# Alternating large and small expert pairs, with a rearranged beginning and end of a mixture-of-experts stage

## The chip, the core and the metric

One core of a Trainium2 chip runs the whole program in one launch. The metric is the device time of one execution in microseconds (us). The engines named below are TensorE (PE in the profile, its weight loads PEld), VectorE (DVE), ScalarE (ACT), GpSimd (POOL) and SyncE (SP), whose queue issues most transfers. SBUF holds tiles of 128 partitions; matmuls write to the eight banks of PSUM.

## What is computed

A model of several layers works on 256 tokens of width 1024, in float32. The change concerns its last stage alone, a mixture of 32 experts with the final norm, cut here to what matters:

```python
logits = hf @ router_w + router_b
top_logit, top_idx = lax.top_k(logits, 4)
gates = softmax(top_logit)                      # 4 experts for each of 256 tokens
gu = x_rows @ w_gu[e] + b_gu[e]                 # 1024 -> 2048
gate, up = min(gu[..., :1024], 7), clip(gu[..., 1024:], -7, 7)
y = ((up + 1) * gate * sigmoid(1.702 * gate)) @ w_down[e] + b_down[e]
x = x + g2 * segment_sum(y * row_gate, row_tok)
out = rms_norm(x) * final_g
```

Every expert's weights are read once: 8.4 MB of w_gu and 4.2 MB of w_down, 402.7 MB for 32 experts.

## The kernel before, in words

`run` (at the end of the file) computes the layers one after another; `moe` (L2077) is the last. All its weights are loaded by SP's queue with `wload` (L146 to L156) into one ring of 16 buffers of about 1 MB (`big`), in the order of the program: eight tiles of w_gu and four of w_down for an expert, 24 tiles for a pair. A buffer is loaded again when the matmuls that read it are done.

The experts are ranked by how many tokens chose them (`moe_route`, L2364), and each rank has a fixed number of rows: experts 0 and 1 come first with 64 rows each, then ranks 2 to 8 with 96, ranks 9 to 16 with 64, ranks 17 to 31 with 32. `pairs` (L2086) puts two ranks together that share one set of up to 128 rows: pair 0 is experts 0 and 1, whose weights are loaded before the ranks are known (`first`, L2089); pairs 1 to 7 are 96 + 32 rows (called large below), pairs 8 to 15 are 64 + 32 (small). They run in this order. An expert's number is read from the tile `orders` into a register of SP (`moe_expert`, L2322), for the address of its weights.

For a pair, `pair` (L2236) makes a matrix that picks the pair's tokens, `gather` (L2197) multiplies it with the normalized tokens, held as a high and a low part (`xn`, made at L2268 to L2271 through a raw copy `xnraw` in the tile `moey`), and ScalarE and VectorE in turn scale the result into `xg`. `up` (L2129) adds the bias with matmuls of a selecting matrix `sel` (L2139 to L2145), which needs the ranks, and then multiplies by w_gu (L2154, recorded as L2126); L2161 to L2165 compute the activation, `down` (L2178) transposes it and multiplies by w_down (also L2126), and L2195 multiplies by the gate vector `moegate`, which `gate_bc` spreads over the partitions (L2110). `put` (L167 to L176) scales the rows by the token's weight and splits them into two parts, `scatter` (L2112) adds them to the residual `X` with matmuls (L2119) and additions (L2121). It runs one pair late. A rank with more tokens than rows is handled by `moe_beyond` (L2324): a branch on all engines over a long body, which reads a flag from `orders` (L2327) and in the measured run is not taken (L2328). In the body stand weight loads into the same ring, matmuls, activations and additions to `X`. After it the final norm: squares (L400), logarithm and exponential (L110, L111) with their activation table preloaded (L2310, recorded as L101), product (L2315) and the write of the output (L2316).

What the order of the instructions is: the tile framework schedules them per engine by what it takes to be ready first, so an instruction without operands can float up; `keep_in_program_order` holds one behind the instruction of its engine traced just before it in the same block. Waits between engines are put in by the framework, by tile. Four PSUM banks rotate under the name `mm`, four under `tp`, in the order in which the program takes them.

Of the kernel before, what the change touches and what calls it, by code (L numbers as in the profile page):

```python
# [50 lines left out]
class Kern:  # L51
# [2025 lines left out]
    def moe(self):  # L2077
# [7 lines left out]

        pairs = [((0, 64), (1, 64))] + [((1 + b, 96 if b < 8 else 64), (32 - b, 32)) for b in range(1, 16)]  # L2086
        rows = dict(chain.from_iterable(pairs))
        most = lambda r: 256 if r < 2 else min(256, 1024 // (r - 1))
        first = [gu_of(0), dn_of(0), gu_of(1)]  # L2089
        with self.pool("moe", 1) as P, self.pool("moew", 1) as W:  # L2090
# [18 lines left out]
            bgu = [P.tile([128, 512], F32, name=f"bgu{i}") for i in "hl"]  # L2109
            gate = self.gate_bc(P, 2, 5, 0, "moegate", tc.keep_in_program_order)  # L2110

            def scatter(gt, ys):  # L2112

                for t in range(2):
                    for h in range(2):
                        hs = slice(h * 512, h * 512 + 512)
                        p = self.ps("tp")
                        for i, v in enumerate(ys):
                            nc.tensor.matmul(p, gt[:, t * 128:(t + 1) * 128], v[:, hs], start=(i == 0), stop=(i == len(ys) - 1))  # L2119
                        x = self.X(2 + t)[:, hs]  # L2120
                        nc.vector.tensor_add(x, x, p)  # L2121
                        yield
# [5 lines left out]

            def up(gu, r, xs):  # L2129


                ps = []
                for x in xs:
                    n = x.shape[2]
                    w = 8 * n
                    pair = [self.ps("mm"), self.ps("mm")]
                    ps.append(pair)
                    sel = W.tile([128, 2, 160], F32, name="moesel", bufs=2)[:, :, :takes[n].shape[2]]
                    nc.gpsimd.tensor_scalar(sel.bitcast(FR), takes[n], own[:, r:r + 1], None, op0=OP.mult)  # L2139
                    for q, p in enumerate(pair):  # L2140
                        for j in range(64 // n):
                            m0 = 0 if n == 64 else 32 - 32 * j
                            for i in range(2):
                                nc.tensor.matmul(p[:, :w], sel[:, q, m0:m0 + 128].bitcast(FR),  # L2144
                                                 bgu[i][:, j * w:(j + 1) * w].bitcast(FR), start=(i == j == 0), stop=False)  # L2145
                step = 8 // len(xs) // 2 if len(xs) > 1 else 8
                for k0 in range(0, 8, step):
                    for x, pair in zip(xs, ps):
                        n = x.shape[2]
                        w, mm = tile_mm(n)  # L2150
                        for k in range(k0, k0 + step):
                            for p, c0 in zip(pair, (0, D)):
                                for c in range(128 // n):
                                    mm(p, c, x[:, k, :], gu(k)[:, c0 + c * w:c0 + (c + 1) * w], False, k == 7)  # L2154
                us = []
# [41 lines left out]
            def gather(x, oh, n):  # L2197

                per = 4 if n > 64 else 8
                for k0 in range(0, 8, per):  # L2200
                    p = self.ps("tp")
                    pv = p[:, :per * n].rearrange("p (k s) -> p k s", k=per)
                    for kk in range(per):
                        ks = slice((k0 + kk) * 128, (k0 + kk + 1) * 128)
                        for i, v in enumerate(xn):
                            for t in range(2):
# [29 lines left out]
            def pair(b):  # L2236
# [5 lines left out]
                for r, n in pairs[b]:  # L2242
                    nc.vector.tensor_tensor(oh[:, :, r0:r0 + n].bitcast(FR), bc(io[:, None, 0:n], [128, 2, n]),
                                            bc(ps_[:, :, r:r + 1], [128, 2, n]), op=OP.is_equal)
                    r0 += n
                xg = W.tile([128, 8, 128], F32, name="xg", bufs=2)[:, :, :m]
                gather(xg, oh, m)
# [16 lines left out]
            with self.pool("moer", 1) as T:  # L2264
# [3 lines left out]
                for t in range(2):  # L2268
                    xr = W.tile([128, D], F32, name="xnraw", tag="moey")
                    nc.scalar.activation(xr, self.X(2 + t), AF.Copy, scale=self.rx[:, t:t + 1])  # L2270
                    self.split(xr, xn[0][:, t, :], xn[1][:, t, :])  # L2271
                route = self.moe_route(T, W, io, pos0, R0, pos, R, G, Ge, own, takes, orders, rows)
# [3 lines left out]
                next(route)  # L2276
                self.split(braw, *bgu)
                gt, tg = next(cur)
            back = iter(())
            for b in range(16):  # L2280
                if b == 1:
                    self.moe_bias(W, Ge, gate)
                y, yh, yl = (W.tile([128, D], F32, name=f"moey{i}")[:sum(n for _, n in pairs[b])] for i in ("", "h", "l"))
                row = 0
                for i, (r, n) in enumerate(pairs[b]):
# [3 lines left out]
                    row += n  # L2289
                    us = up(gu, r, [xg[:, :, q] for q in rs])  # L2290

# [6 lines left out]
                    down(dn, us, [y[q] for q in rs])  # L2298
                self.put((yh, yl), y, tg[:, 1:2])
                back = scatter(gt.bitcast(FR), [yh.bitcast(FR), yl.bitcast(FR)])  # L2300
# [3 lines left out]
            fg = W.tile([128, D], F32, name="fing", tag="moey")  # L2304
            nc.sync.dma_start(fg, bass.AP(tensor=a["final_g_2"].tensor, offset=a["final_g_2"].offset, ap=[[0, 128], [1, D]]))
            for _ in back:
                pass
            self.moe_beyond(rows, most, orders, gu_of, dn_of, overflow)

            self.ln_exp()  # L2310
            with self.pool("moef", 1) as F:
                xs = [self.X(2), self.X(3)]
                r = self.row_rms(F, xs)
                for t in range(2):
                    nc.vector.scalar_tensor_tensor(xs[t], xs[t], r[:, t:t + 1], fg, op0=OP.mult, op1=OP.mult)  # L2315
                    nc.sync.dma_start(a["out"][t * 128:(t + 1) * 128], xs[t])  # L2316

# [237 lines left out]
```

## Time and profile before

| | us |
|---|---|
| median of 3 runs (lowest, highest) | 3098.86 (3097.3, 3103.04) |
| profiled execution, its own time | 3102.66 |
| its span, first to last instruction | 3100.9 |
| TensorE busy | 2765.1 (89%), mean granted clock 0.916 |
| VectorE busy | 1490.4 (48%) |
| ScalarE busy | 882.5 (28%) |
| GpSimd busy | 517.4 (17%) |
| transfers | 650.74 MB, mean 210 GB/s |

Times count from the start of the span. A busy TensorE is not TensorE at its peak: its matmuls overlap, and their ends are modelled. The granted clock is a share of 2.4 GHz, averaged over a stretch; single instructions run at 1.2 or 2.4 GHz. The DMA share is the mean over 16 engines and goes a little over 1 where packets overlap. A wait is put down to what released it last. A line can be a helper's.

### The profile page before, as it was taken

The numbers are of one execution on the slowest core, as the hardware profiler recorded it, in microseconds if no ns is written. First come the engines' busy times: TensorE is split into PE (matmuls) and PEld (weight loads), VectorE is DVE, ScalarE is ACT, GpSimd is POOL, SyncE is SP. The second block draws the span as 40 slices with busy tenths as digits, with TensorE's granted clock in tenths as the row PEclk, the third lists the DMA queues.
The fourth block names the chain that finished last, engine by engine and source line by source line (L and its number), as shares of the span: only waits on it lengthen the run. The fifth ranks groups of instructions, "written<-read, shape, count | busy, mean of one in ns | idle before, by whom it ended". The sixth has DMA issues, their size and how long they took to land. (4 is left out here: it accounts for less than half of the span.)

```text
span 3100.9 us, 47594 instructions
## 1 busy us (share of the span) xinstructions
PE 2765.1 (89%) x19070; PEld 1795.3 (58%) x19070; DVE 1490.4 (48%) x3210; ACT 882.5 (28%) x1827; POOL 517.4 (17%) x774
## 2 busy tenths in 40 slices
PE   7998989999979788987899988989999999998775
PEld 4873468888847555654798966763444433443332
DVE  4426465555567655764655878651222222222121
ACT  4223334223235343433454634530100000000001
POOL 0002310111100543543100322111100000000000
PEclk9998999999988897887899998989999999879887
DMA  6226741233221233432456323369999999999997
GB/s 227 96 92 211 273 144 55 95 95 95 86 86 42 75 108 98 108 95 81 144 190 204 118 62 113 125 248 360 381 411 382 373 377 372 416 417 416 416 417 290
DMA packets 254007, 650.74 MB, mean 210 GB/s; under 512 B 68816, under 2 KB 129616, under 8 KB 215376
## 3 DMA queue, kind: packets, MB, share of 16 engines
q1 hardware_dynamic: 239552, 632.96, 55.4%
q10 hardware_dynamic: 12432, 10.45, 1.1%
q0 software_dynamic: 1792, 4.20, 0.5%
q8 instruction: 152, 2.49, 0.3%
q14 instruction: 79, 0.65, 0.1%
HBM read 639.16 MB, written 8.39 MB: 209 GB/s over the span
## 5 line engine op out<-in xcount | busy, mean ns | idle before, releaser
L2126 PE MATMUL mm<-w,xg 128*32 128x256 f32 (+1 forms) x3904 | 434.2, 457 | 38.3 <-DMA w<-in_moe_w_gu_dram 38.3
L164 DVE TENSOR_TENSOR lo<-w,hi 128x512 fp32r<-128x512 f32 (+1 forms) x330 | 295.1, 927 | 107.7 <-ACT hi L163 93.4
L2126 PEld LDWEIGHTS mm<-w,xg 128*32 128x32 f32 (+1 forms) x3904 | 155.7, 120 | 306.0 <-issue 190.2
L163 ACT ACTIVATE hi<-w 128x512 fp32r<-128x512 f32 (+1 forms) x356 | 256.3, 770 | 236.5 <-PE tp L250 101.2
L2126 PE MATMUL mm<-w,moeaT 128*32 128x256 f32 (+1 forms) x1952 | 258.7, 500 | 8.7 <-DVE moeaT L95 3.8
L2162 ACT ACTIVATE moes<-moeg 128x256 f32<-128x256 f32 (+1 forms) x39 | 19.9, 510 | 653.6 <-DVE moeg L2161 653.6
L2161 DVE TENSOR_SCALAR moeg<-mm 128x256 f32<-128x256 f32 (+1 forms) x39 | 21.1, 541 | 349.7 <-PE mm L2126 349.3
L250 PE MATMUL mm<-mlo,hi 128*128 128x512 f32 (+1 forms) x512 | 173.4, 339 | 0.7 <-DVE mlo L173 0.7
L249 PE MATMUL mm<-mhi,hi 128*128 128x512 f32 (+1 forms) x512 | 173.1, 340 | 0.0
L251 PE MATMUL mm<-mhi,lo 128*128 128x512 f32 (+1 forms) x512 | 172.2, 337 | 0.0
L2126 PEld LDWEIGHTS mm<-w,moeaT 128*32 128x32 f32 (+1 forms) x1952 | 79.8, 128 | 140.8 <-issue 108.8
L251 PE MATMUL tp<-hi,aTl 128*128 128x512 f32 x384 | 151.7, 395 | 0.0
L250 PE MATMUL tp<-lo,aTh 128*128 128x512 f32 x384 | 151.3, 394 | 0.0
L249 PE MATMUL tp<-hi,aTh 128*128 128x512 f32 x384 | 151.1, 393 | 0.0
L2164 POOL TENSOR_TENSOR moeg<-moeg,moes 128x256 f32<-128x256 f32 (+1 forms) x39 | 37.4, 959 | 580.6 <-ACT moes L2162 566.0
L2195 DVE TENSOR_TENSOR moey<-mm,moegate 32x256 f32<-32x256 f32 (+1 forms) x122 | 60.5, 496 | 138.8 <-PE mm L2126 127.3
L164 POOL TENSOR_TENSOR lo<-w,hi 128x512 fp32r<-128x512 f32 (+1 forms) x26 | 51.8, 1994 | 348.0 <-ACT hi L163 293.9
L250 PEld LDWEIGHTS mm<-mlo,hi 128*128 128x128 f32 x512 | 96.4, 188 | 12.8 <-DVE mlo L173 1.1
L249 PEld LDWEIGHTS mm<-mhi,hi 128*128 128x128 f32 x512 | 96.0, 188 | 12.3 <-issue 0.5
L251 PEld LDWEIGHTS mm<-mhi,lo 128*128 128x128 f32 x512 | 96.3, 188 | 11.4
L2139 POOL TENSOR_SCALAR moesel<-moetk,moeown 128x320 fp32r<-128x320 f32 (+1 forms) x39 | 40.8, 1046 | 317.3 <-PE mm L2144 278.0
L249 PE MATMUL cv<-hT2h,hi 128*128 128x256 f32 x288 | 84.3, 293 | 8.8 <-DVE cvy L1754 8.8
(866 smaller groups left out, 5897.8 us busy)
## 6 DMA issues: line engine op xcount, KB each, us to landing
w<-in_moe_w_gu_dram SPq DMA_DIRECT2D x256, 1024.0 KB, 15.0
w<-in_moe_w_down_dram SPq DMA_DIRECT2D x128, 1024.0 KB, 16.6
w<-in_mlp_w_dram SPq DMA_DIRECT2D x64, 1024.0 KB, 5.4
w<-in_ada_w_dram SPq DMA_DIRECT2D x48, 1024.0 KB, 5.0
w<-in_w_in_dram SPq DMA_DIRECT2D x26, 1024.0 KB, 5.2
adaw<-in_ada_w_dram SPq DMA_DIRECT2D x48, 512.0 KB, 4.1
w<-in_ab_w_in_dram SPq DMA_DIRECT2D x14, 1024.0 KB, 5.1
w<-in_rw_w_rkv_dram SPq DMA_DIRECT2D x8, 1024.0 KB, 5.1
```

Source lines behind the costliest of these rows:

```text
L163: nc.scalar.activation(h, raw, AF.Copy)
L164: (eng or nc.vector).tensor_sub(l, raw, hi)
L249: nc.tensor.matmul(out, l[0], r[0], start=start, stop=False)
L250: nc.tensor.matmul(out, l[0], r[1], start=False, stop=False)
L251: nc.tensor.matmul(out, l[1], r[0], start=False, stop=stop)
L2126: return 8 * n, lambda p, c, l, r, s, st: nc.tensor.matmul(p[c * n:(c + 1) * n, :8 * n], l, r, start=s, stop=st, tile_position=(0, c * n))
L2139: nc.gpsimd.tensor_scalar(sel.bitcast(FR), takes[n], own[:, r:r + 1], None, op0=OP.mult)
L2161: nc.vector.tensor_scalar(g, pg[:, :w], 7.0, None, op0=OP.min)
L2162: nc.scalar.activation(s, g, AF.Sigmoid, scale=1.702)
L2164: nc.gpsimd.tensor_mul(g, g, s)
L2195: nc.vector.tensor_mul(y[:, cs], py[c * n:(c + 1) * n, :w], gate[c * n:(c + 1) * n, cs])
```

## The change

1. `pairs`: after pair 0 the others run in the order 8, 1, 9, 2, 10, 3, 11, 4, 12, 5, 13, 6, 14, 7, 15 of the old numbers, a small and a large one in turn.
2. The tokens' high part comes straight from the scaled copy on ScalarE, the low part from one operation on VectorE (scale and subtract), placed behind the first selecting matrix. `gather` takes all high parts of a PSUM tile before the low parts.
3. The gate's matmuls and copies stand behind the routing.
4. For the very first expert the bias matmuls stand behind the weights' matmuls.
5. `moe_beyond` stands ahead of the last pair.
6. In the last pair `put` goes by column halves, and `scatter` by column halves in every pair.
7. The table preload stands ahead of the last scatter; the final product is two operations, the one with `final_g` ahead of the norm's factor, into two tiles, with the second tile's last operation on ScalarE.

```diff
-        pairs = [((0, 64), (1, 64))] + [((1 + b, 96 if b < 8 else 64), (32 - b, 32)) for b in range(1, 16)]
+        pairs = [((0, 64), (1, 64))] + [((1 + b, 96 if b < 8 else 64), (32 - b, 32))
+                                        for b in (8, 1, 9, 2, 10, 3, 11, 4, 12, 5, 13, 6, 14, 7, 15)]
...
-            gate = self.gate_bc(P, 2, 5, 0, "moegate", tc.keep_in_program_order)
-
             def scatter(gt, ys):
-                for t in range(2):
-                    for h in range(2):
+                for h in range(2):
+                    for t in range(2):
...
-            def up(gu, r, xs):
+            def up(gu, r, xs, late=False):
...
-                                                 bgu[i][:, j * w:(j + 1) * w].bitcast(FR), start=(i == j == 0), stop=False)
+                                                 bgu[i][:, j * w:(j + 1) * w].bitcast(FR), start=not late and (i == j == 0),
+                                                 stop=late and i == 1 and j == 64 // n - 1)
+
+                for x in xs:
+                    pair = [self.ps("mm"), self.ps("mm")]
+                    ps.append(pair)
+                    if not late:
+                        bias(x.shape[2], pair)
...
-                                    mm(p, c, x[:, k, :], gu(k)[:, c0 + c * w:c0 + (c + 1) * w], False, k == 7)
+                                    mm(p, c, x[:, k, :], gu(k)[:, c0 + c * w:c0 + (c + 1) * w], late and k == 0, k == 7 and not late)
+                if late:
+                    for x, pair in zip(xs, ps):
+                        bias(x.shape[2], pair)
...
-                    for kk in range(per):
-                        ks = slice((k0 + kk) * 128, (k0 + kk + 1) * 128)
-                        for i, v in enumerate(xn):
+                    for i, v in enumerate(xn):
+                        for kk in range(per):
+                            ks = slice((k0 + kk) * 128, (k0 + kk + 1) * 128)
...
+                if b == 0:
+                    for t in range(2):
+                        nc.vector.scalar_tensor_tensor(xn[1][:, t, :].bitcast(FR), self.X(2 + t), self.rx[:, t:t + 1], xn[0][:, t, :],
+                                                       op0=OP.mult, op1=OP.subtract)
...
-                    xr = W.tile([128, D], F32, name="xnraw", tag="moey")
-                    nc.scalar.activation(xr, self.X(2 + t), AF.Copy, scale=self.rx[:, t:t + 1])
-                    self.split(xr, xn[0][:, t, :], xn[1][:, t, :])
+                    nc.scalar.activation(xn[0][:, t, :].bitcast(FR), self.X(2 + t), AF.Copy, scale=self.rx[:, t:t + 1])
...
                 self.split(braw, *bgu)
+                gate = self.gate_bc(P, 2, 5, 0, "moegate", tc.keep_in_program_order)
...
+                if b == 15:
+                    self.moe_beyond(rows, most, orders, gu_of, dn_of, overflow)
...
-                    us = up(gu, r, [xg[:, :, q] for q in rs])
+                    us = up(gu, r, [xg[:, :, q] for q in rs], b == i == 0)
...
-                self.put((yh, yl), y, tg[:, 1:2])
+                for hs in (slice(0, 512), slice(512, 1024)) if b == 15 else (slice(0, D),):
+                    self.put((yh[:, hs], yl[:, hs]), y[:, hs], tg[:, 1:2])
...
+            self.ln_exp()
             for _ in back:
                 pass
-            self.moe_beyond(rows, most, orders, gu_of, dn_of, overflow)
-
-            self.ln_exp()
             with self.pool("moef", 1) as F:
...
-                    nc.vector.scalar_tensor_tensor(xs[t], xs[t], r[:, t:t + 1], fg, op0=OP.mult, op1=OP.mult)
-                    nc.sync.dma_start(a["out"][t * 128:(t + 1) * 128], xs[t])
+                    xf = W.tile([128, D], F32, name="xf", tag="moey" + "hl"[t])
+                    nc.vector.tensor_mul(xf, xs[t], fg)
+                    if t:
+                        nc.scalar.activation(xf, xf, AF.Copy, scale=r[:, t:t + 1])
+                    else:
+                        nc.vector.tensor_scalar(xf, xf, r[:, t:t + 1], None, op0=OP.mult)
+                    nc.sync.dma_start(a["out"][t * 128:(t + 1) * 128], xf)
```

## Rows read from the trace of the kernel before

**Rows 1.** Page, part 2: GB/s moved, the span in 40 equal slices.
```profile
GB/s 227 96 92 211 273 144 55 95 95 95 86 86 42 75 108 98 108 95 81 144 190 204 118 62 113 125 248 360 381 411 382 373 377 372 416 417 416 416 417 290
```

**Rows 2.** Stretches: span; busy of PE, PEld, DVE, ACT, POOL; clock, DMA share, GB/s.
```profile
2080.00:2100.00 20.00, 19.58 (x82) 12.19 (x84) 8.76 (x24) 4.76 (x8) 4.52 (x7) 0.67 0.24 79
2150.00:2200.00 50.00, 48.26 (x376) 20.22 (x375) 11.79 (x22) 3.04 (x7) 8.68 (x8) 0.93 0.79 300
2300.00:2600.00 300.00, 274.88 (x2450) 119.58 (x2450) 75.85 (x159) 21.49 (x41) 26.26 (x27) 0.94 0.93 373
2600.00:3060.00 460.00, 385.83 (x2755) 173.59 (x2748) 104.15 (x218) 34.38 (x60) 29.90 (x30) 0.88 1.02 416
```

**Rows 3.** Waits of SP's queue, 2303 to 2600: us in total, times, longest.
```profile
SPq L155 <- PE mm L2126: 225.2, 102, 9.9
```

**Rows 4.** Timeline of PE: first weights of pairs 6, 7, 8, 9; start, length.
```profile
2480.43 1.94 PE L2126 MATMUL mm<-w,xg 128*64 128x512 f32 x8
...
2509.15 13.36 PE L2126 MATMUL mm<-w,moeaT 128*64 128x512 f32 x94
...
2549.28 2.94 PE L2126 MATMUL mm<-w,xg 128*64 128x512 f32 x24
...
2615.34 1.94 PE L2126 MATMUL mm<-w,xg 128*64 128x512 f32 x8
...
2663.62 2.80 PE L2126 MATMUL mm<-w,xg 128*64 128x512 f32 x12
```

**Rows 5.** Timeline of PE, beginning of the stage: gather, first weights, pair 1's bias.
```profile
2080.28 0.47 PE L2207 MATMUL tp<-moeoh,xnmh 128*128 128x128 f32 x1 [0.77 <-ACT xnmh L163]
...
2086.71 0.63 PE L2207 MATMUL tp<-moeoh,xnml 128*128 128x128 f32 x2
...
2090.85 15.07 PE L2126 MATMUL mm<-w,xg 128*64 128x512 f32 x64
...
2145.82 0.50 PE L2144 MATMUL mm<-bguh,moesel 128*128 128x512 f32 x1
```

**Rows 6.** Timeline of ACT, beginning of the stage: copy of the second token tile.
```profile
2078.00 1.13 ACT L2270 ACTIVATE xnraw<-Xl,routr 128x1024 f32<-128x1024 f32 x1
```

**Rows 7.** Timeline of DVE, beginning: rank comparison, reader of the rank places.
```profile
2081.51 1.23 DVE L2436 TENSOR_TENSOR routab<-routkey 128x1024 f32<-128x1024 f32 x1
...
2089.09 0.23 DVE L2398 SCALAR_TENSOR_TENSOR moepos<-mm,routselr 128x64 f32<-128x64 f32 x1 [1.18 <-PE mm L2396]
```

**Rows 8.** The branch's line: operation, count, duration min/median/max in ns, first and last start.
```profile
L2328 PEldq COMPARE_BRANCH  x1: 4865/4865/4865, 3082.6 to 3082.6; - x1
...
L2328 SPq EVENT_SEMAPHORE  x9: 17/17/17, 3086.1 to 3089.0; - x9
```

**Rows 9.** Waits, 3060 to 3101: us in total, times, longest.
```profile
ACT rms_junk L400 <- DVEq L2328: 7.5, 1, 7.5
```

**Rows 10.** Timeline of all engines, the end.
```profile
3076.59 1.07 PE L2126 MATMUL mm<-w,moeaT 128*32 128x256 f32 x16 [0.22 <-DMA w<-in_moe_w_down_dram]
...
3077.73 1.73 DVE L2195 TENSOR_TENSOR moey<-mm,moegate 32x256 f32<-32x256 f32 x4 [6.70 <-PE mm L2126]
...
3080.67 1.28 DVE L176 SCALAR_TENSOR_TENSOR moeyl<-moey,moetg,moeyh 96x1024 fp32r<-96x1024 f32 x1 [1.22 <-ACT moeyh L175]
...
3083.22 2.48 DVE L2121 TENSOR_TENSOR Xl<-Xl,tp 128x512 f32<-128x512 f32 x4 [1.27 <-PE tp L2119]
...
3088.14 1.06 ACT L400 ACTIVATE rms_junk<-Xl 128x1024 f32<-128x1024 f32 x1 [7.50 <-DVEq L2328]
...
3090.49 1.28 ACT L110 ACT_TABLE_LOAD   x1
...
3094.32 2.48 DVE L2315 SCALAR_TENSOR_TENSOR Xl<-Xl,rms_r,fing 128x1024 f32<-128x1024 f32 x2
```

**Rows 11.** DMA issues: KB each, median us from issue to landing.
```profile
w<-in_ada_w_dram SPq DMA_DIRECT2D x48, 1024.0 KB, 5.0
```

**Rows 12.** Timeline of ACT: the preloaded table before.
```profile
2091.45 1.28 ACT L101 ACT_TABLE_LOAD   x1 [0.72 <-DVE moeord L2469]
```

More of the change, by code (lines that the diff above doesn't have):

```diff
@@ L2127, in tile_mm, with bias @@
                                                                          tile_position=(0, c * n))
-            def up(gu, r, xs):
+            def up(gu, r, xs, late=False):
                 ps = []
-                for x in xs:
-                    n = x.shape[2]
+                def bias(n, pair):
                     w = 8 * n
-                    pair = [self.ps("mm"), self.ps("mm")]
-                    ps.append(pair)
                     sel = W.tile([128, 2, 160], F32, name="moesel", bufs=2)[:, :, :takes[n].shape[2]]
```

## The prediction

> **What bounds it now.** I read the slices of the page first: from the twenty-eighth (2093 us) on, the transfer rate stands at 360 to 417 GB/s, but for the last one with the end in it [rows 1]. That is the last stage, the mixture of experts, from about 2080 us to the end; nothing of the change touches what lies before. The stretches [rows 2] show three things there. From 2600 to 3060 us the 16 DMA engines are full (share 1.02, 416 GB/s): a tile of 1.0486 MB takes 2.52 us, so a pair of two experts (24 tiles) takes 60.5 us, whatever the engines do. Between 2300 and 2600 us the rate is only 373, between 2150 and 2200 only 300, and from 2080 to 2100 it is 79. Against 416 that is 300 x (1 - 373/416) = 31, 50 x (1 - 300/416) = 14 and 20 x (1 - 79/416) = 16 us of transfer lost, 61 us in all.
>
> Why it is lost in the middle, the waits of SP's queue tell: from 2303 to 2600 us its weight loads wait 225 us, in 102 waits, for TensorE to give a buffer back [rows 3]. The starts of the pairs' first weights [rows 4] give TensorE's own time. A large pair (96 + 32 rows) took 2549.28 - 2480.43 = 68.9 and 2615.34 - 2549.28 = 66.1 us, more than its 60.5 us of transfer; the first small pair (64 + 32) took 2663.62 - 2615.34 = 48.3 while its weights still lay ready. So seven large pairs in a row are TensorE's, eight small ones in a row are the transfers', and the faster side can't save more than 16 tiles (40 us) for later.
>
> **The taking of turns.** A large and a small pair together need 114 to 117 us of TensorE and 121 us of transfer: the transfers become the bound if their lead never fills the 16 buffers. Count it in tiles. At the first matmul 16 are loaded. Pair 0 takes TensorE 55.0 us (2090.85 to 2145.82 [rows 5]), in which 21.8 tiles come for 24 used: lead 14. The first small pair takes off (60.5 - 48.3)/2.52 = 4.8: lead 9. A large pair adds at most 8.4/2.52 = 3.3, and the next small one takes 4.8 off again. Within a large pair the first expert (12 tiles) lasts from 2480.43 to 2522.51 [rows 4], time for 16.7 tiles, so the lead is up to 4.7 higher in its middle: the highest point is at the first large pair, 9 + 4.7, still under 16. I keep 2 us of loss for that and take the other 43 of the 45 us back. Bounds: 36 (TensorE slower, below) to 45.
>
> **The beginning.** Weights stop at about 2079 us because TensorE uses none before 2090.85 [rows 5]. Ahead of that stand the gather, from 2080.28 to 2087.34, the copies into xg and the four matmuls of the first bias. In the trace the second token tile's scaled copy starts only at 2078.00 on ScalarE [rows 6], behind the tile that both halves share, and the rank comparison, which writes into that same tile, only at 2081.51 on VectorE [rows 7]. With the raw copy gone both can run at 2073 to 2075. But the changed order has a limit of its own: the gate's two PSUM tiles are now taken after the routing's, so that the first weights' second PSUM tile is the one of the rank places, whose reader ended the chain at 2089.09 [rows 7]. That chain is the comparison, a sum of like length, four short operations, the places' matmuls and this reader; it took 2089.3 - 2081.5 = 7.8 us. Begun at 2074 to 2077, among two low parts of 1.28 us each and the xg copies, it ends at 2083 to 2087. I take 2085 for the first weights, 6 us earlier; bounds 0 (the chain is delayed as it was) and 9 (the end of a gather begun at 2074 that lasts the 7 us it lasts now). The bias itself is moved, not saved. As all later transfers follow one another, the gain passes on in full.
>
> **The general branch.** Ahead of pair 15 it costs more than at the end. At the end its price is seen: TensorE's branch lasts 4.87 us and SP has nine semaphore steps at it [rows 8]; the squares of the last norm wait until 3088.14 for VectorE to be past the branch, though the last addition ended at 3083.22 + 2.48 = 3085.70 [rows 9, 10]. The reason is that the skipped body writes the same tile: what comes behind it waits for the engine that might have written it. The body also loads weights, and more tiles than there are buffers. So ahead of pair 15 the load of every one of its tiles has to wait until TensorE, which might have read that buffer in the body, is past the branch, and until then no transfer runs. I cost it as TensorE's lag behind the last tile of pair 14, plus the branch, plus the refilling of the queue. The lag: a large pair needs 6 to 8 us more than its transfers, and the last tile's work is another 1.1 [rows 10], so 8 to 9. The branch: 5.0. The refill: a load of 1 MB into an empty queue lands 5.0 us after its issue, where little else runs [rows 11], 2.5 more than in a stream. Together 17 us (taken). Lower bound 0 (loads not held), upper 25 (lag of a lead that has not run out: some 3 tiles more). The steps on VectorE, ScalarE, GpSimd and SP lie beside TensorE's and cost nothing while it is behind; if it is not, SP's own wait for its loads to land is inside the lag.
>
> The Trainium skill, Advanced Engine Details and Errata, section Control Flow Timing, gives about 108 ns for a compare-and-branch. By that the term would be 12 us, not 17; the row of 4865 ns decides.
>
> **The end.** After the last matmul (3077.66) stand now: the gate products of 1.73, the scaled high copy, the low part of 1.28 until 3081.95, then four additions until 3085.70 [rows 10]. In halves, the high copy of the first half runs beside the products of the second and the second half's low part of about 0.64 (half of 1.28) is all that stands behind it: the additions end at about 3083.4, 2.3 less. The squares need no branch: 2.4 less. The preloaded table stands behind the last copy, so the two table loads of 1.28 go: 2.6 less. In the trace the same preload ran at 2091.45 and was undone long before the end, since the activations of the experts need another table [rows 12]; it now has the last copy ahead of it in its own block and cannot float there. The last product of 2.48 for both tiles becomes a copy of some 1.2 on two engines at once, 1.2 less, while the two products with the final gain (1.28 each) stand on VectorE beside the squares and the logarithm; their weight arrives about a microsecond after the squares would want it, so I give 0.5 back. Sum 8; bounds 5 and 9.
>
> From the first of these loads to the last product 3.83 us pass, 2.57 of them the two loads [rows 10]. The Trainium skill, ScalarE: Activation LUTs, section What ACT_TABLE_LOAD costs, counts a drain of about 1.38 us on top of each load; by that the end would gain 2.8 us more, but in 3.83 us two drains have no room.
>
> **Sum.** -43 - 6 + 17 - 8 = -40 us. The profiled execution took 3102.66 us, so 3062.7; it stands 3.8 above the median of the runs, 3098.86, which gives 3059. A measurement of this kernel can tell about 0.2% (6 us) from no change.
>
> **Rivals.**
> *The branch is nearly free* (the loads of pair 15 get past it, or TensorE has no lag there): 3059 - 17 = 3042. For it: no row shows a weight load behind a branch. Against: [rows 9] show the hold for another tile. 0.17.
> *TensorE remains the bound in part.* Its granted clock is 0.88 where it is starved and 0.94 where it is not [rows 2]. If small pairs keep the starved clock in the new order, a small pair takes 48.3 x 0.94/0.88 = 51.6 and a large one, at the 68.9 of [rows 4], makes 120.5: no slack, the lead stays near full, and the loads stall in each large pair as in 2300 to 2600. Then perhaps half of the 45 is got back and the branch finds a full lead: 3059 + 20 = 3079. Against: with weights ready TensorE does not starve. 0.12.
> *Slower: the lower clock all along.* If the turns kept TensorE often at 1.2 GHz, the pairs behind pair 0 (7 x 66 + 8 x 48.3 = 848 us) would set the end. No change is reached when the last matmul ends 8 us (the gain of the end) after 3077.66: from 2085, with 55 for pair 0 and 5 for the branch, that leaves 941 us, 11% more than 848, a mean clock of 0.94/1.11 = 0.85. At 0.80 they take 848 x 0.94/0.80 = 996, 55 us slower than now: 3154. Against: no long stretch is below 0.88 [rows 2]. 0.04.
> *An edit that does nothing*: the preload may float again; +2.6, inside the range.
>
> **How the numbers follow.** My forecast (3046 to 3074 with its bounds) has 0.67. The free branch with a good beginning gives 3059 - 17 - 6 = 3036; the part-bound case reaches 3080. So 3036 to 3080. Faster by over 0.2%: 0.67 + 0.17 + 0.09 = 0.93; slower 0.04; within 0.2%, by the worst of the part-bound case (all loads stalled and no gain at the beginning), 0.03.
>
> **What would show it.** Right: in the stretches, full transfers from about 2090 us to the branch; SP's queue waiting for TensorE only in the first pairs; one hole of 15 to 20 us in the transfers some 60 us ahead of the last weights; the first weights' matmul near 2085; no table load between the last squares and the logarithm. Wrong: transfers below 400 GB/s across a large pair in the middle (second rival); no hole at the branch (first); a mean clock below 0.85 (third); a first matmul still at 2090.

## The result, and the profile after

The changed kernel takes 3069.5 us (median of 4 runs, 3066.32 to 3076.67) against 3100.95 us (4 runs, 3097.3 to 3106.97) of the kernel before on the same chip: ratio 0.9895, 95% interval 0.9874 to 0.9915. It is about 1% faster, with the interval clear of 1, and the time lies in the range, 10 us above the forecast of 3059.

The runs of one kernel differ by 10 us and more in what lies ahead of the stage, where the code is the same. So the stage is measured by itself: from the copy of the norm factors on VectorE (L1670, the tile `routr`), which no part of the change touches, to the end of the span. It starts at 2069.05 us in the trace of before and at 2072.88 in that of after. The stage has three parts: to the first weights' matmul, from there to the end of the last weights' matmul, and from there to the end. All in us:

| kernel | stage | to first weights | weights | behind the last matmul |
|---|---|---|---|---|
| before | 1031.8 | 21.8 | 986.8 | 23.2 |
| after | 1002.0 | 20.5 | 965.1 | 16.4 |

29.8 us are gained, not 40: 1.3 of them at the beginning, 21.7 in the weights, 6.8 at the end.

**The turns.** The first fence is part 2 of the page of after (GB/s in 40 slices of the span), the second four stretches of after (start and end; length; busy us of PE, PEld, DVE, ACT, POOL; clock, DMA share, GB/s). The last stretch is the neighbourhood of the branch.

```profile
GB/s 229 92 85 215 279 150 56 96 96 95 84 77 54 67 116 95 102 89 103 119 192 192 130 90 116 76 270 327 390 411 417 415 418 415 417 416 417 416 309 332
```

```profile
2096.00:2346.00 250.00, 232.12 (x1710) 102.50 (x1708) 58.80 (x122) 19.98 (x38) 25.29 (x24) 0.95 1.01 404
2300.00:2600.00 300.00, 269.07 (x2315) 121.17 (x2313) 73.59 (x157) 23.21 (x44) 24.52 (x26) 0.94 1.02 416
2600.00:2960.00 360.00, 324.50 (x2661) 147.88 (x2658) 90.00 (x190) 27.79 (x53) 28.43 (x29) 0.91 1.02 416
2965.00:3005.00 40.00, 32.33 (x298) 15.57 (x294) 13.67 (x27) 1.56 (x2) 2.71 (x3) 0.91 0.53 211
```

The sag to 373 of [rows 1, 2] is gone: 416 GB/s from 2300 to 2960 us, in large and small pairs alike. In the first 250 us it is 404, which is 250 x (1 - 404/416) = 7 us lost, and around the branch 40 x (1 - 211/416) = 19.7 us. The waits of SP's queue for TensorE from 2300 to 2600 us (us in total, times, longest) are no longer those of [rows 3]:

```profile
SPq L155 <- PE mm L2126: 59.3, 41, 5.8
```

SP still waits for TensorE 41 times, but 59 us instead of 225. The rate of this stretch is 416 GB/s all the same, so these waits cost nothing here: it is the rate of the stretch that decides.

**The beginning.** VectorE, then TensorE (start, length) with a stretch of 20 us from the copy of the factors (columns as above), and behind them two rows of VectorE and one of TensorE in the kernel before for the same steps:

```profile
2072.88 0.16 DVE L1670 COPY routr<-rms_r 128x2 f32<-128x2 f32 x1
...
2078.16 1.20 DVE L2454 TENSOR_TENSOR routab<-routkey 128x1024 f32<-128x1024 f32 x1
2079.29 0.48 DVE L2251 TENSOR_TENSOR moeoh<-moeio,moepos 128x128 fp32r<-128x128 f32 x2
```

```profile
2075.20 0.63 PE L2412 MATMUL mm<-routsele,routbf 128*128 128x32 f32 x2 [2.73 <-DVE routsele L2406]
...
2079.91 2.15 PE L2215 MATMUL tp<-moeoh,xnmh 128*128 128x128 f32 x9 [2.07 <-DVE moeoh L2251]
...
2089.03 3.76 PE L389 MATMUL mm<-adat,ident 128*128 128x512 f32 x4
...
2093.39 13.95 PE L2126 MATMUL mm<-w,xg 128*64 128x512 f32 x64
...
2149.40 0.50 PE L2142 MATMUL mm<-bguh,moesel 128*128 128x512 f32 x1
```

```profile
2072.88:2092.88 20.00, 15.54 (x63) 12.82 (x63) 14.18 (x56) 6.32 (x12) 5.72 (x10) 0.50 0.45 167
```

```profile
2069.05 0.16 DVE L1670 COPY routr<-rms_r 128x2 f32<-128x2 f32 x1
...
2073.33 0.47 DVE L2243 TENSOR_TENSOR moeoh<-moeio,moepos 128x128 fp32r<-128x128 f32 x2
```

```profile
2068.47 1.96 PE L389 MATMUL mm<-adat,ident 128*128 128x512 f32 x4
```

The selecting matrix comes 6.4 us behind the copy of the factors, 2.1 later than before (2073.33 - 2069.05 = 4.3). VectorE takes the rank comparison (1.20) ahead of it now, and the routing's matmuls took 0.63 where the same two took 0.41 before, behind 2.7 us of idling, where the gate's matmuls used to run ahead of them. TensorE's granted clock stays at 0.50 (1.2 GHz, the lower of its two levels) for the whole 20 us behind the copy (0.68 in the same 20 us before). The gather starts 7.0 behind the copy; before, its first two matmuls ran at 4.9 and the others from 11.2 on [rows 5]. It ends 14.6 behind the copy instead of 18.3. But between it and the first weights now stand the gate's four matmuls, and at this clock they take 3.76 us; before, ahead of all this, they took 1.96. And the pair 1 bias, the first step behind pair 0, starts 2149.40 - 2072.88 = 76.5 us behind the copy against 76.8 before. In the other runs with the same code up to there it starts at 75.5 to 76.9, so it can't be told whether any of the 1.3 us is left by then.

**The branch.** Stretches of 5 us (columns as above), then the rows of the branch's line (duration min/median/max in ns, first and last start), SP's wait for the first load behind it, and the timeline of PE and SP:

```profile
2970.00:2975.00 5.00, 5.00 (x57) 2.84 (x50) 3.90 (x8) 0.00 (x0) 0.00 (x0) 1.00 0.63 255
2975.00:2980.00 5.00, 5.00 (x84) 2.91 (x87) 1.28 (x2) 0.00 (x0) 0.00 (x0) 1.00 0.40 161
2980.00:2985.00 5.00, 2.80 (x42) 1.58 (x38) 2.33 (x8) 0.42 (x1) 0.72 (x1) 0.93 0.01 3
2985.00:2990.00 5.00, 4.48 (x60) 2.19 (x52) 0.44 (x2) 0.00 (x0) 0.00 (x0) 0.73 0.02 7
2990.00:2995.00 5.00, 1.71 (x6) 1.38 (x7) 2.79 (x4) 1.15 (x1) 1.99 (x2) 0.95 0.24 36
```

```profile
L2346 SPq EVENT_SEMAPHORE  x9: 17/17/17, 2969.3 to 2979.8; - x9
...
L2346 PEldq EVENT_SEMAPHORE  x2: 51/51/51, 2992.1 to 2992.2; - x2
L2346 DVEq EVENT_SEMAPHORE  x2: 21/21/21, 2993.0 to 2993.1; - x2
L2346 SPq COMPARE_BRANCH  x1: 53/53/53, 2964.1 to 2964.1; - x1
...
L2346 PEldq COMPARE_BRANCH  x1: 3406/3406/3406, 2988.6 to 2988.6; - x1
L2346 DVEq COMPARE_BRANCH  x1: 72/72/72, 2990.2 to 2990.2; - x1
```

```profile
SPq L155 <- DVEq L2346: 13.1, 1, 13.1
```

```profile
2984.13 5.35 PE L2126 MATMUL mm<-w,moeaT 128*32 128x256 f32 x64 [0.31 <-DVE moetg L2267]
...
2993.26 4.36 SPq L155 DMA_DIRECT2D w<-in_moe_w_gu_dram  x8
...
2998.32 1.94 PE L2126 MATMUL mm<-w,xg 128*64 128x512 f32 x8 [0.56 <-DMA w<-in_moe_w_gu_dram]
```

SP reaches the branch at 2964.1 and stays in it until the loads that it has issued have landed, at 2979.8 (its last semaphore step). TensorE comes to the branch at 2988.6, 8.8 us behind that landing, and ends pair 14 at 2984.13 + 5.35 = 2989.5, 9.7 behind it. Then its branch; VectorE's semaphore steps follow at 2993.0; 0.2 us later SP issues the first load of pair 15, which had waited for VectorE (13.1 us). So VectorE is the last to be past the branch: its compare-and-branch took only 72 ns, but it came to it 1.6 us behind TensorE, and its semaphore steps followed 2.8 us later. The first weights are used 5.1 us behind that, at 2998.3.

**The end.** Timeline of all engines:

```profile
3057.37 1.07 PE L2126 MATMUL mm<-w,moeaT 128*32 128x256 f32 x16 [0.93 <-DMA w<-in_moe_w_down_dram]
...
3061.03 1.28 ACT L101 ACT_TABLE_LOAD   x1
...
3064.35 1.06 ACT L400 ACTIVATE rms_junk<-Xl 128x1024 f32<-128x1024 f32 x1 [2.04 <-DVE Xl L2121]
...
3066.84 1.22 DVE L2329 TENSOR_TENSOR xf<-Xl,fing 128x1024 f32<-128x1024 f32 x1
...
3067.97 0.15 DVE L112 TENSOR_TENSOR rms_t<-rms_r 128x2 f32<-128x2 f32 x1
```

The table is loaded once, right behind the last scaled copy and ahead of the squares; no load stands between squares and root as in [rows 10]. The squares start 5.9 us behind the end of the last matmul, 10.5 before.

### The profile page after: what moved, and what is told of

Same layout as the page of the kernel before. It is cut to its first block, busy times and chain, and to the rows that moved or that the text cites. A ratio compares the mean times of both kernels' runs of the same rounds, so it can differ in the third digit from the quotient of the medians.

```text
span 3074.8 us, 47587 instructions
## 1 busy us (share of the span) xinstructions
PE 2762.5 (90%) x19070; PEld 1800.2 (59%) x19070; DVE 1495.1 (49%) x3212; ACT 877.9 (29%) x1825; POOL 515.8 (17%) x774
## 5 line engine op out<-in xcount | busy, mean ns | idle before, releaser
L2126 PE MATMUL mm<-w,xg 128*32 128x256 f32 (+1 forms) x3904 | 423.0, 449 | 15.9 <-DMA w<-in_moe_w_gu_dram 15.9
L2126 PE MATMUL mm<-w,moeaT 128*32 128x256 f32 (+1 forms) x1952 | 258.9, 491 | 10.9 <-ACT moeaT L97 4.4
L2170 ACT ACTIVATE moes<-moeg 128x256 f32<-128x256 f32 (+1 forms) x39 | 19.9, 509 | 641.9 <-DVE moeg L2169 641.9
L250 PEld LDWEIGHTS mm<-mlo,hi 128*128 128x128 f32 x512 | 96.3, 188 | 12.6 <-DVE mlo L173 1.0
## 6 DMA issues: line engine op xcount, KB each, us to landing
w<-in_moe_w_down_dram SPq DMA_DIRECT2D x128, 1024.0 KB, 19.9
```

The lines of the kernel that those rows point to most:

```text
L250: nc.tensor.matmul(out, l[0], r[1], start=False, stop=False)
L2126: return 8 * n, lambda p, c, l, r, s, st: nc.tensor.matmul(p[c * n:(c + 1) * n, :8 * n], l, r, start=s, stop=st, tile_position=(0, c * n))
L2170: nc.scalar.activation(s, g, AF.Sigmoid, scale=1.702)
```

## The experiments

All were timed beside the kernel before on the same chip. The stage and its parts, as above:

| kernel | median us, runs | ratio, interval | stage | to first weights | weights | behind |
|---|---|---|---|---|---|---|
| branch at the end | 3053.39, 4 | 0.9878, 0.9837 to 0.9919 | 989.4 | 20.5 | 948.4 | 20.6 |
| turns alone | 3057.32, 4 | 0.9891, 0.9854 to 0.9927 | 991.8 | 22.6 | 946.5 | 22.8 |
| all but the turns | 3108.78, 10 | 1.0022, 0.9999 to 1.0044 | 1035.1 | 20.5 | 998.1 | 16.5 |
| gate after first weights | 3071.02, 1 | | 1002.0 | 17.1 | 968.6 | 16.3 |
| branch behind last down | 3051.44, 4 | 0.982, 0.9789 to 0.985 | 989.2 | 20.5 | 948.7 | 20.0 |
| branch ahead of the fourth pair | 3072.71, 1 | | 1012.5 | 20.5 | 975.6 | 16.3 |
| small pair ahead of the branch | 3059.9, 1 | | 1004.6 | 20.5 | 967.7 | 16.4 |
| bias at the tenth pair | 3056.93, 4 | 0.9857, 0.9822 to 0.9892 | 986.7 | 20.5 | 946.3 | 19.9 |
| changed kernel again | 3070.5, 6 | 0.988, 0.9857 to 0.9904 | 1002.2 | 20.5 | 965.4 | 16.3 |
| branch behind last down again | 3053.43, 6 | 0.9828, 0.9804 to 0.9851 | 989.2 | 20.5 | 948.7 | 20.0 |

The medians scatter with what lies ahead of the stage (the copy of the factors stood anywhere from 2053.5 to 2084.9 us in the profiled runs); the stage of one kernel came out alike in two runs, within 0.3 us. Its parts scatter more: to the first weights, the kernel before took 21.8 us and the turns alone, with the same code there, 22.6. By the medians alone the first kernel of the table (0.9878) isn't told from the changed one (0.9895); by the stage it is.

**Branch at the end.** The changed kernel with the branch, and the preload behind it, where they were.

```diff
-                if b == 15:
-                    self.moe_beyond(rows, most, orders, gu_of, dn_of, overflow)
...
-            self.ln_exp()
             for _ in back:
                 pass
+            self.moe_beyond(rows, most, orders, gu_of, dn_of, overflow)
+
+            self.ln_exp()
```

> The changed kernel with the general branch and the table preload back behind the last scatter. Theory (the hole in the transfers ahead of pair 15 comes from the loads waiting for the branch): no hole, transfers at 415 GB/s to the last weights, 20 us less there; the end gets 5 us longer again (2.4 for the branch, 2.6 for two table loads): some 15 us below the changed kernel, about 45 below the one before. Rival (TensorE's lag would have made the hole without a branch): less than 8 us below the changed kernel, and loads that wait for TensorE there.

The weights take 948.4 us, 16.7 less than in the changed kernel, and the end 4.2 more. So the place of the branch costs 12.6 us net, of some 15 expected, and the loads' wait for the branch makes the hole: without it there are full transfers around the same place (416 GB/s from 2955 to 2995 us). ScalarE at its end (timeline):

```profile
3042.51 1.28 ACT L110 ACT_TABLE_LOAD   x1
3043.80 0.20 ACT L110 ACTIVATE rms_t<-rms_v 128x2 f32<-128x2 f32 x1
3044.02 1.28 ACT L111 ACT_TABLE_LOAD   x1
```

The preload is undone again, as in [rows 12], and both tables are loaded: the part of the end that keeps the table in place hangs on what stands ahead of it in its block. The Trainium skill (ScalarE: Activation LUTs, What ACT_TABLE_LOAD costs) counts a drain of about 1.38 us on top of each load. No run here shows one: the load of 1.28 that starts at 3042.51 ends at 3043.79, and the next operation starts at 3043.80.

**Turns alone.** The kernel before with the new `pairs`, nothing else (the first part of the diff).

> The kernel before with the new order of the pairs and nothing else. Theory (the turns give back the stalls in the large pairs): 41 us below the kernel before, 2300 to 2600 us at 415 GB/s. Rival (the turns are worth little without the other edits): less than 20 us below.

The stage is 40.0 us shorter, the weights' part 40.3, and from 2300 to 2600 us the rate is 416 GB/s. That is nearly the whole of what the order can give (45, less 5 to 7 lost in the first pairs). Beside the kernel above it also prices the new beginning: that one reaches its first weights 2.05 us earlier and then takes 1.9 us longer for the weights.

**All but the turns.** The changed kernel with `pairs` of before.

```diff
-                                        for b in (8, 1, 9, 2, 10, 3, 11, 4, 12, 5, 13, 6, 14, 7, 15)]
+                                        for b in range(1, 16)]
```

> The changed kernel with the old order of the pairs. Ahead of pair 15 stand starved small pairs, so TensorE has hardly any lag. Theory (hole = lag + branch + refill): a hole of 9 to 12 us, the beginning 1 and the end 7 us shorter than before: 0 to 5 us above the kernel before. Rival (a fixed price of some 20 us for a branch ahead of loads): 11 to 13 us above it.

The stage is 3.3 us longer than before: the hole takes more than beginning and end give. Here pair 14 is a small one, and TensorE has hardly any lag: it comes to the branch 0.6 us behind the last landing. The hole (stretch of 40 us around the branch, columns as above) is 40 x (1 - 302/416) = 11 us:

```profile
3015.00:3055.00 40.00, 28.73 (x170) 11.34 (x170) 7.77 (x17) 1.56 (x2) 2.70 (x3) 0.70 0.74 302
```

**Gate after the first weights.** One line moved: `gate` is made behind the first expert's `up`.

```diff
-                gate = self.gate_bc(P, 2, 5, 0, "moegate", tc.keep_in_program_order)
...
                     us = up(gu, r, [xg[:, :, q] for q in rs], b == i == 0)
+                    if b == i == 0:
+                        gate = self.gate_bc(P, 2, 5, 0, "moegate", tc.keep_in_program_order)
```

> The changed kernel with the gate's matmuls behind the first expert's weights, so that they and the rank places' PSUM tile no longer stand ahead of them. In the changed kernel the first weights start 20.5 us after the copy of the norm factors (L1670). If TensorE's own queue holds them: 17 to 18.5. If the copies into xg hold them (they end 19.2 after it): 19 to 20. If the PSUM tile of the rank places holds them: about 16.6, where its reader ends. The time moves by the same 0 to 4 us, too little for one look.

The copy of the factors starts at 2067.20 here. TensorE, then the same gather of pair 1 in the changed kernel:

```profile
2084.30 16.04 PE L2126 MATMUL mm<-w,xg 128*64 128x512 f32 x64
...
2101.31 1.88 PE L389 MATMUL mm<-adat,ident 128*128 128x512 f32 x4
2102.62 1.39 PE L2215 MATMUL tp<-moeoh,xnmh 128*128 128x96 f32 x8
```

```profile
2108.32 0.99 PE L2215 MATMUL tp<-moeoh,xnmh 128*128 128x96 f32 x8
```

The first weights come 17.1 us behind the copy, 3.4 earlier, so the gate's matmuls in TensorE's own queue were what held them. But the stage is 1002.0, as in the changed kernel. Pair 1's gather starts 2102.62 - 2067.20 = 35.4 us behind the copy, in the changed kernel 2108.32 - 2072.88 = 35.4 as well: the 3.4 us are gone by then. Two things took them. The gate's matmuls now stand behind the first expert's, where they put the gather back by 1.3. And the first expert's 64 matmuls took 16.04 us instead of 13.95, 2.1 more: in the 5 us from the first weights on the granted clock is 0.58, in the changed kernel 1.00, where it rises with the first weights (0.50 up to 2092.88, 0.90 from there to 2095.38). So what starts earlier here runs longer at the lower clock. The rate in the first 250 us behind the first weights is 398 GB/s, not 404. While the buffers are full, TensorE sets the pace, and moving work within its queue, from ahead of the first weights to behind them, gained nothing here.

**Branch behind the last down matmuls.** The branch stands behind the last expert's `down`, ahead of the last `put`; the preload keeps its place.

```diff
-                if b == 15:
-                    self.moe_beyond(rows, most, orders, gu_of, dn_of, overflow)
...
                     down(dn, us, [y[q] for q in rs])
+                    if b == 15 and i == 1:
+                        self.moe_beyond(rows, most, orders, gu_of, dn_of, overflow)
```

> The changed kernel with the general branch behind the last pair's last products and ahead of its split into two parts: no weight load stands behind it, and the table preload stays behind it and ahead of the last scatter. Theory (the whole price is the loads' waiting): no hole, 415 GB/s to the last weights; the stretch from the last weights' matmul to the end, 16.4 us in the changed kernel and 20.6 with the branch at the end, is 18 to 20, since the branch's 3 to 5 us lie partly beside the split: 16 to 18 us below the changed kernel. Rival (a branch with work in flight costs the same anywhere): an end of 25 us or more.

No load is left to be held, and the weights take 948.7 us. The end is 20.0: the branch costs 3.6 there, since the last scatter waits for VectorE to be past it (its first matmul, at 3041.17, for 5.5 us). The stage is 12.8 us shorter than that of the changed kernel, a few us less than expected: the hole costs 16.4 of its 19.7. It is also, within 0.2 us, the stage with the branch at the end (989.4): where no load is left to be held, the place of the branch made no difference.

**Branch ahead of the fourth pair.** `b == 15` becomes `b == 3`; again a large pair stands ahead of it, but an early one.

> The changed kernel with the general branch ahead of the fourth pair instead of the last. There TensorE lags far behind the transfers (SP's loads still wait for buffers). Theory (hole = TensorE's lag + branch + refill): a hole of 35 to 50 us, and the stage from the copy of the norm factors to the end, 1002 us in the changed kernel, 1017 to 1032. Rival (a fixed price of some 20 us): 1000 to 1005.

The branch's line, the first weights' matmuls of the 32-row expert ahead of it, and the stretch around it:

```profile
L2346 SPq EVENT_SEMAPHORE  x9: 17/17/17, 2236.3 to 2236.9; - x9
...
L2346 PEldq COMPARE_BRANCH  x1: 3361/3361/3361, 2254.3 to 2254.3; - x1
```

```profile
2237.26 1.07 PE L2126 MATMUL mm<-w,xg 128*32 128x256 f32 x16
```

```profile
2225.00:2265.00 40.00, 33.24 (x331) 17.04 (x330) 12.29 (x27) 2.48 (x4) 4.12 (x4) 0.88 0.34 129
```

The loads have landed at 2236.9 and TensorE comes to the branch only at 2254.3, 17 us later, since it has more loaded tiles before it. The hole is 40 x (1 - 129/416) = 27.6 us. The stage, 1012.5, is 10.5 us above that of the changed kernel: the right direction, but less than the lag theory expected. The lead was not short: when the last load landed, all 12 tiles of the 32-row expert were still unused (its first weights' matmul starts at 2237.26), which agrees with the 9 and more of the prediction's count. But TensorE went through them in 17.4 us, 1.45 for a tile, faster than the 2.52 of a transfer.

**Small pair ahead of the branch.** The large pair of each turn goes first, so that pair 14 is small.

```diff
-                                        for b in (8, 1, 9, 2, 10, 3, 11, 4, 12, 5, 13, 6, 14, 7, 15)]
+                                        for b in (1, 8, 2, 9, 3, 10, 4, 11, 5, 12, 6, 13, 7, 14, 15)]
```

> The changed kernel with the turns begun by a large pair, so that two small pairs come last and the branch stands behind a small one. Theory (hole = lag + branch + refill, and a starved small pair leaves no lag): a hole of 9 to 12 us in place of 20, partly paid for at the beginning, where a large pair meets a full lead (3 to 8 us more stalls there): the stage from the copy of the norm factors 994 to 1002 us. Rival (fixed price): a hole of 20 and 1002 to 1010.

The branch's line, and the first 250 us and the neighbourhood of the branch:

```profile
L2346 SPq EVENT_SEMAPHORE  x9: 17/17/17, 2959.0 to 2971.6; - x9
...
L2346 PEldq COMPARE_BRANCH  x1: 3966/3966/3966, 2972.2 to 2972.2; - x1
```

```profile
2077.00:2327.00 250.00, 233.81 (x1740) 106.35 (x1738) 60.16 (x128) 20.25 (x39) 26.55 (x25) 0.91 0.96 386
2950.00:2990.00 40.00, 28.78 (x257) 13.41 (x255) 10.46 (x21) 1.56 (x2) 3.75 (x3) 0.87 0.75 303
```

TensorE is at its branch 0.6 us behind the last landing (2971.6), and the hole is 40 x (1 - 303/416) = 10.9 us, as expected. The stage is longer, not shorter, than that of the changed kernel (1004.6, outside what was expected): with a large pair at the head the first pairs lose 250 x (1 - 386/416) = 18 us instead of 7. The order of a turn moved the stall from one end to the other: 11 us more at the head, 9 less at the branch.

**Bias at the tenth pair.** The kernel with the branch behind the last down matmuls, and `moe_bias`, the bias of w_down, made in pair 9 instead of pair 1.

```diff
-                if b == 1:
+                if b == 9:
```

> The kernel of the branch behind the last down products, with the down projection's bias (moe_bias) moved from the second pair to the tenth. In the second pair the buffers are full, so its 4.7 us of TensorE and 1.5 us of waiting hold the loads; at the tenth TensorE has time to spare. If the early stalls of the transfers (7 us within 250 us of the first weights) come from TensorE's work there: 4 to 7 us less stall and as much off the time. Rival (they come from something else, or the bias only stalls elsewhere): 0 to 2 us.

In the changed kernel this step stands in the first expert of pair 1 (timeline of PE), with a wait for its own load; the second fence is the first 250 us without it:

```profile
2159.15 4.69 PE L2376 MATMUL tp<-moebd,moeGT 32*128 32x512 f32 x8 [1.54 <-DMA moebd<-in_moe_b_down_dram]
```

```profile
2084.00:2334.00 250.00, 230.86 (x1718) 101.74 (x1714) 57.30 (x120) 20.62 (x39) 21.24 (x21) 0.94 1.01 411
```

The first pairs lose 250 x (1 - 411/416) = 3 us; with the branch alone moved they lose 6 in the same stretch (406 GB/s, from 3.4 us behind the first weights on). From 2600 to 2720, around the tenth pair, the rate is 411, which is 1.4 us lost there. The stage is 2.5 us shorter than with the branch alone moved, between what the theory (4 to 7) and its rival (0 to 2) expected, and the medians don't show it. What the 3 us left are was not tried.

**Both once more.** The changed kernel, unaltered, and the one with the branch behind the last down matmuls, on one chip.

> The changed kernel itself, unaltered, beside the next one on the same chip. Theory (the branch ahead of the last pair costs 16.5 us net in the weights' stretch and gives 4 back at the end): ratio to the kernel before 0.989 to 0.992, stage from the copy of the norm factors to the end 1001 to 1004 us, hole at the branch 18 to 21 us.

> The kernel with the branch behind the last pair's down matmuls, once more, on the same chip as the changed kernel. Theory: 10 to 15 us below the changed kernel (0.3 to 0.5%), ratio to the kernel before 0.984 to 0.988, stage 988 to 991 us, first transfers lost at the branch only those of the end. Rival (the earlier 0.982 was the chip's part ahead of the stage): medians within 6 us of the changed kernel, though the stage is shorter.

The medians are 17 us apart, 3070.5 and 3053.43, and the intervals of the ratios don't touch; the stages are 13.0 apart. The difference of the medians is more than was expected, and both ratios lie just below what was expected; the stages, 1002.2 and 989.2, are as expected. The 40 us around the branch in the changed kernel's repeat, and 40 us in the same part of the other kernel, which has no branch there:

```profile
2960.00:3000.00 40.00, 32.97 (x298) 16.32 (x294) 13.41 (x27) 1.56 (x2) 3.77 (x3) 0.87 0.56 223
```

```profile
2965.00:3005.00 40.00, 36.09 (x328) 15.14 (x327) 10.97 (x25) 2.11 (x4) 2.53 (x3) 0.87 1.02 417
```

The hole of the repeat is 40 x (1 - 223/416) = 18.6 us, where the first trace had 19.7: a hole is known to about 1 us. The version with the branch behind the last down matmuls beats both kernels: 0.9828 of the time before.

## Why the prediction was right, and where it was off

It was right in sign and range; its likeliest case happened, and the sum of the terms was 10 us too large. Measured in the stage, term by term:

| term | predicted | measured | from |
|---|---|---|---|
| turns | -43 | -39.5 | turns alone against before, up to the last matmul |
| beginning | -6 | -0.2 | branch at the end against turns alone, up to the last matmul |
| branch ahead of pair 15 | +17 | +16.7 | after against branch at the end, weights |
| end | -8 | -6.8 | after against before, behind the last matmul |
| sum | -40 | -29.8 | after against before |

**The beginning** is the step that failed, in both of its halves. "I take 2085 for the first weights": on the clock of the trace before they came at 2090.85 - 1.3 = 2089.6. The gather did end earlier, but the gate's matmuls stood between it and the weights; I had looked at who holds the PSUM tile (the rank places) and not at what else was put into TensorE's queue. The experiment with the gate moved shows it: there the first weights come at what would be 2069.05 + 17.1 = 2086.1 on that clock. Nor did I look at the granted clock: with the gate's matmuls gone from ahead of the routing it was 0.50 up to the first weights, and the gate's matmuls took 3.76 us there instead of 1.96. "The gain passes on in full" failed too: 3.4 us at the first weights left the stage unchanged, and the changed kernel's start of weights, 2.05 us ahead of that of the turns alone, left 0.2 at the last matmul. Transfers set the end only later; in pair 0 the loaded buffers are ready and TensorE is the bound, so what was only moved within its queue gave nothing, and part of what started earlier ran at the lower clock. The lower bound, 0, held.

**The turns** were right in mechanism: full rate across large and small pairs from 2300 us on. The 2 us that I kept for a full lead were 5 to 7. The lead is at its highest in the first pairs, and my count left out the bias of w_down, 4.69 + 1.54 us of TensorE's time in pair 1: without it there the loss was 3 instead of 6. The rival of a bound in part (373 would have stayed) and that of a lower clock (0.94 and 0.91 in the two long stretches) are out.

**The branch** was right in its mechanism, the loads held until the engines are past it. That its size came out as 16.7 for 17 is in part luck, since errors of some us in its parts made up for each other. The parts that I had were near: a lag of 9.7 (8 to 9), 3.8 from TensorE's end to the first load (5.0), 5.1 from there to the first weights (5.0, of which 2.5 counted). TensorE came to the branch 0.6, 8.8 and 17.4 us behind the last landing (small pair ahead, the changed kernel, fourth pair), and the holes are 10.9, 19.7 and 27.6 us: the lag and some 10 to 11 us more, at all three places (with all but the turns, 0.6 and 11.0). The Trainium skill (Advanced Engine Details and Errata, Control Flow Timing) gives about 108 ns for a compare-and-branch; TensorE's took 3406 ns and VectorE's 72, by the trace, and the term of 12 us that the page would have made is not what came. But it was not TensorE's branch that let the first load go. "The steps on VectorE, ScalarE, GpSimd and SP lie beside TensorE's and cost nothing while it is behind" was wrong: VectorE's semaphore steps were the last, 0.9 us behind TensorE's, so by this trace a shorter branch on TensorE alone would not have brought the load forward. And the sum didn't hold that the loads ahead of the branch thin out as they end (255 and 161 GB/s), 2.0 + 3.1 = 5 us. Of the 19.7 us 3 come back at the end of the kernel: with the branch behind the last down matmuls the last loads thin out there too (329 and 237 GB/s in the two stretches of 5 us ahead of the last four: 3.2 us lost), in the changed kernel they don't (410 and 408 there). The rival of a free branch is out.

**The end** gave 6.8 of 8. Up to the squares it went as worked out (4.6 of 4.7). Behind them it gave 2.3 instead of 3.3: the second product with `final_g` (3066.84, 1.22) stands on VectorE ahead of the first step of the root (3067.97), which had its input at 3067.4, and the first one had waited 0.7 for its weight, as I had half allowed. From the end of the last product to the end of the span it takes 4.8 us instead of 4.1, which I had not counted.

Of what I said would show it, the hole of 15 to 20 us and the missing table loads came; the first weights near 2085 did not, nor a full rate from 2090 on; a first matmul still at 2090, my sign for a wrong beginning, came true with 2089.6; and SP's waits for TensorE did not stop, they only ceased to cost anything.

## What to carry to other kernels

A branch over a body that might touch a shared ring of buffers is paid for where it stands: here every later load was held until the slowest engine was past it. So put it where no load is left to issue, here behind the last weights' matmuls or, as good, at the end where it had been. When two resources take turns at being the bound, mixing the kinds of work can be worth more than all work on their edges (39.5 us here, against 6.8 at the end and 0.2 at the beginning), less what is lost where the queue between them still fills (5 to 7 us). Moving work off the way to a first instruction gained nothing here, since it stayed in the queue that was the bound; and where the clock starts low, read the clock beside the start, since what begins earlier may run longer.

## What the runs showed of the hardware

- The compare-and-branch over the skipped body took 3.4 to 4.9 us on TensorE in all traces, and 50 to 72 ns on the other engines. On VectorE, ScalarE and GpSimd the semaphore step at its line then followed 2.4 to 3.9 us later (VectorE after the change: 2990.2 to 2993.0).
- A long stream of loads didn't end at its full rate. Page part 2 of a window of after, 2940 to 2985 us in 40 slices of 1.1 us: mean busy tenths of the 16 DMA engines. Behind it 5 us of the kernel with the small pair ahead of the branch.

```profile
DMA  9999999999999999999999999996655555100000
```

```profile
2965.00:2970.00 5.00, 4.69 (x51) 1.88 (x49) 1.00 (x5) 0.00 (x0) 0.00 (x0) 0.66 0.59 238
```

SP was done issuing at 2952.38 + 9.97 = 2962 (its queue's timeline), but the share falls to 0.6 and 0.5 from about 2970 on and stays there for some 8 us. The rate falls in step with the share (255/0.63 = 405 and 161/0.40 = 403 GB/s, 416/1.02 = 408 in the full stream), so the engines were idle for part of this time and no slower when busy. It is not TensorE's lag that does it: with the small pair ahead of the branch TensorE is only 0.6 us behind, and the loads ahead of the branch thin out alike (238 GB/s from 2965 to 2970, the last landing at 2971.6). The loads of pair 15 behind the hole, some 60 us of transfer, did not thin out (410 and 408 GB/s near their end). Why this is so was not tried.
